# Samples' value products in rounds of four quarters, and the prompt's forget sums by tiles, in a fused two-layer encoder step

## The chip, the cores and the metric

The kernel runs on one core of one Trainium2 chip. The metric is the device time of one execution in microseconds (us). The engines are named as in the profile: PE is TensorE (matmul), PEld its weight loads, DVE VectorE, ACT ScalarE, POOL GpSimd, SP the engine that only issues DMAs. A time in the timeline is counted from the first instruction of the execution.

## The reference, cut to what matters

Two layers: a gated MLP with spatial mixing, then attention with a forget gate. Two request groups share the weights: a prompt of 512 rows, and 8 samples of 16 new rows, each with 256 cached rows of keys and values. There are 16 heads of 128. The change lies in the attention layer:

```python
def fox_attend_prompt(q, k, v, logf):
    cT = jnp.cumsum(logf, axis=1).transpose(0, 2, 1)      # running sums, per head
    ...
        s = jnp.einsum('bqhd,bkhd->bhqk', qi, k).astype(jnp.float32) * scale
        s = s + ci[..., :, None] - cT[:, :, None, :]
    ...

def fox_attend_sample(q, k_new, v_new, logf_new, k_cache, v_cache, logf_cache):
    k = jnp.concatenate([k_cache.astype(k_new.dtype), k_new], axis=1)
    v = jnp.concatenate([v_cache.astype(v_new.dtype), v_new], axis=1)
    ...
    p = jax.nn.softmax(s, axis=-1).astype(v.dtype)
    return jnp.einsum('bhqk,bkhd->bqhd', p, v).reshape(B, T, H * dh)
```

## The kernel before

All 640 rows (512 of the prompt, 128 of the samples) go through the layers together, as five tiles of 128. Large products are made from three products of halves: `mm3` splits each f32 operand into a high and a low part and adds high by high (L272), high by low (L273) and low by high (L274). The parts are written by `split`: ScalarE copies the high part (L289), VectorE subtracts it for the low part (L290, or L293 with a scale). The projections of the attention layer use seven products in place of eight (`seven_products`), whose operands are built by GpSimd (L211) and whose sums VectorE adds (L713 to L729).

The attention layer runs over eight pairs of heads. For each pair p the projections of the gate z of p and of v, k and q of p + 1 are a sequence of steps on TensorE, and pieces of attention are laid between them by written due times (`interleave`, `prompt_times`, `sample_times`). The program is then ordered by a scheduler that simulates the engines: an instruction is issued when it is ready in that simulation, unless `issue_after` ties it behind another. So the order around an edit can move too.

The prompt's pieces of a head are `scores`, `turn` (transposes of the softmax rows, L1186) and `values` (L1193), four blocks of 128 rows each. The samples' pieces of a pair and of a group of four samples are `scores` (L1243), `turn` (L1262), `values` (L1267 and L1270) and `gate` (L1277). A product of 32 output rows occupies one quarter of a PSUM bank's partitions; `bl` counts the four samples of a group, one to a quarter. `values` begins with one product over all 128 rows for the new rows' values, and then adds eight products of 32 rows for the cached values (two tiles t of 128 cached rows, four samples). So there are 16 executions of it, two to a pair.

`forget_sums` makes the running sums of the forget gate: four f32 products, one for each tile t of the prompt, with 16 rows (heads) as output and 512, 384, 256 and 128 columns. ScalarE copies them out (L1007), and they go to DRAM as `c_sc`, from where `load_w0` spreads one head's 512 sums over 128 partitions, once for each head. The first such load follows the store at once; its reader is VectorE's L1159. The samples' mask (`cs_sc`) is stored and loaded in the same place. At this place the program is in the projection of k and q of the first pair; L1016 and L1009 belong to the samples' sums, L1099 is the last step of `project_k0`, and L290 on `A` is the low half of a right operand, built from `sums[0]`.

Of the kernel before, what the change touches and what calls it, by code (L numbers as in the profile page):

```python
# [17 lines left out]
F32 = mybir.dt.float32  # L18
F32R = mybir.dt.float32r
AF = mybir.ActivationFunctionType  # L20
# [4 lines left out]
P = 128  # L25
D = 1024
E = 2048
H = 16
DH = 128
SEQ = 512  # L30
# [27 lines left out]
def hybrid_trunk(tc, x_prompt, x_sample, ck, cv, clf, p_prompt, p_sample, norm_pre, norm_post,  # L58
                 g_win, ln_g, ln_b, w_s, b_s, g_wout, f_win, b_f, f_wout, w_proj, w_gate, consts,
                 y_p, y_s, st_v, fk_p, fv_p, fl_p, fk_s, fv_s, fl_s):  # L60
    nc = tc.nc
# [7 lines left out]
    dram = tc.alloc_tile_pool(name="dram", bufs=1, space=DRAM)  # L69
# [13 lines left out]
    PB = [psum.tile([P, 512], F32, name=f"pb{i}") for i in range(8)]  # L83
    x_sc = dram.tile([NT, P, D], F32, name="x_sc")
    y_sc = dram.tile([H, P, TOK], F32, name="y_sc")
    c_sc = dram.tile([H, SEQ], F32, name="c_sc")
    cs_sc = dram.tile([P, 272], F32, name="cs_sc")
    rs_sc = dram.tile([16, P], F32, name="rs_sc")

    def r1(o, n, p=P):  # L90
        return R1[:p, o:o + n]
# [28 lines left out]
    def dma(out, in_, queue=None):  # L120
        if queue is not None:
            queue.dma_start(out=out, in_=in_)
        else:
            behind["sp"] = nc.sync.dma_start(out=out, in_=in_)
# [155 lines left out]
    tri = CST[:, C_TRI:C_TRI + 512]  # L280
# [332 lines left out]
    for p in range(4):  # L613
# [3 lines left out]
        out = v_out if p == 0 else [bank((0, 1, 2, 3, 4, 5, 6, 7)) for _ in range(NT)]  # L617
# [305 lines left out]
    o_KT, o_K, o_V, o_q, o_k, o_vk = 0, 2176, 3200, 5248, 6528, 7808  # L923
    o_P, o_PT, o_v, o_qp = 9088, 10112, 11136, 13696
# [27 lines left out]
    n = NT * H  # L952
    fx, fa, fe, fl, fu, lft = (r1(o_V + 1280 + z * n, n) for z in range(6))
    lf3 = lft.rearrange("p (t h) -> p t h", t=NT)
    fx3 = fx.rearrange("p (t h) -> p t h", t=NT)
    cT, ex, cS = r1(o_PT + 288, SEQ, H), r1(o_PT + 800, P), r1(o_V + 1760, 272)
    assert o <= o_K and o_PT + 288 >= o_P + 1280 and o_PTs + 96 >= o_qp + 1280

    def whole(i, j):
# [43 lines left out]
    def forget_sums():  # L1003
        pb = bank(ATT)
        for t in range(4):
            nc.tensor.matmul(pb[:H, t * P:], lf3[:, t], tri[:, :SEQ - t * P], start=(t == 0), stop=(t == 3))
        nc.scalar.activation(out=cT, in_=pb[:H, :], func=AF.Copy)  # L1007
        dma(c_sc, cT, nc.scalar)
        nc.vector.tensor_tensor(  # L1009
            out=ex.rearrange("p (r b h) -> p r b h", r=NB, b=NB),  # L1010
            in0=blk.rearrange("p (b r h) -> p r b h", b=NB, h=2),
            in1=lf3[:, 4, :].rearrange("p (r h) -> p r h", h=2).unsqueeze(2).broadcast_to([P, NB, NB, 2]), op=ALU.mult)
        pb = bank(ATT)
        nc.tensor.matmul(pb[:, :272], cr[:, 0], tri[:, :272], start=True, stop=False)
        nc.tensor.matmul(pb[:, P:272], cr[:, 1], tri[:, :272 - P], start=False, stop=False)
        nc.tensor.matmul(pb[:, 256:272], ex, CST[:, C_T16:C_T16 + TS], start=False, stop=True)  # L1016
        nc.scalar.activation(out=cS, in_=pb[:, :272], func=AF.Copy)
        behind["act"] = nc.scalar.dma_start(out=cs_sc, in_=cS)
        with queued("act"):
            load_w0(0, nc.scalar)  # L1020


    def v_of(p):
        return r1(o_v + (p % 2) * 1280, 1280).rearrange("p (t n) -> p t n", t=NT)
# [108 lines left out]
    def w0_of(h):  # L1133
        return tri if h % 2 else SF[:, 2048:2560] if h < 14 else r1(o_raw, 512)

    def load_w0(h, queue=None):
        dma(w0_of(h), c_sc[h].partition_broadcast(P), queue)

    def prompt_pieces(h):

# [60 lines left out]
    vv = r1(o_V, 2048).rearrange("p (b t n) -> p b t n", b=4, t=2)  # L1201
# [28 lines left out]
    def sample_pieces(p, bg):  # L1230

        pr = r1(o_Ps, 400)
        pt = r1(o_PTs, 384)
        os_ = r1(o_Ps, 256)
        kept = {}

        def scores():
            S = bank(ATT)
            with queued("dve"):
                nc.vector.tensor_tensor(out=Wc[:, PAST:], in0=Wc[:, PAST:], in1=CST[:, C_M16:C_M16 + TS], op=ALU.add)  # L1240
            for hh in range(2):
                for bl in range(4):
                    nc.tensor.matmul(S[32 * bl:32 * bl + 32, :272], qpads[:, hh, 4 * bg + bl].rearrange("p h q -> p (h q)"),  # L1243
                                     kt[:, hh, bl], start=(hh == 0), stop=(hh == 1))
            m, sm, ri = small(), small(), small()
            nc.vector.tensor_tensor_reduce(out=pr[:, :272], in0=S[:, :272], in1=Wc, scale=1.0, scalar=3e38, op0=ALU.add,
                                           op1=ALU.min, accum_out=m)
            nc.scalar.activation(out=pr[:, :272], in_=pr[:, :272], func=AF.Exp, scale=-1.0, bias=m, accum_out=sm)
            if 2 * p + bg < 15:
                load_mask(2 * p + bg + 1, nc.scalar)  # L1250
            nc.vector.reciprocal(out=ri, in_=sm)
            kept["ri"] = ri

            nc.vector.tensor_tensor(
                out=pr[:, 272:].rearrange("p (b k) -> p b k", b=NB),
                in0=CST[:, C_SEL + bg * P:C_SEL + (bg + 1) * P].rearrange("p (b k) -> p b k", b=NB),
                in1=pr[:, PAST:272].unsqueeze(1).broadcast_to([P, NB, TS]), op=ALU.mult)

        def turn():
            tb = bank(ATT)  # L1260
            for j, o_ in enumerate((0, P, 272)):
                nc.tensor.transpose(out=tb[:, j * P:(j + 1) * P], in_=pr[:, o_:o_ + P], identity=ident)  # L1262
            nc.scalar.activation(out=pt, in_=tb[:, :384], func=AF.Copy)

        def values():
            O = bank(ATT)
            nc.tensor.matmul(O[:, :256], pt[:, 256:], v_of(p)[:, 4], start=True, stop=False)  # L1267
            for t in range(2):
                for bl in range(4):
                    nc.tensor.matmul(O[32 * bl:32 * bl + 32, :256], pt[:, t * P + 32 * bl:t * P + 32 * bl + 32],  # L1270
                                     vv[:, bl, t], start=False, stop=(t == 1))
            nc.scalar.activation(out=os_, in_=O[:, :256], func=AF.Copy, scale=kept["ri"])

        def gate():
            tb = bank(ATT)
            for hh in range(2):
                nc.tensor.transpose(out=tb[:, hh * P:(hh + 1) * P], in_=os_[:, hh * P:(hh + 1) * P], identity=ident)  # L1277
            for hh in range(2):
                h = 2 * p + hh
                cs = slice(512 + 64 * bg, 512 + 64 * bg + 64)  # L1280
                y = y_of(h)[:, cs].rearrange("p (b q) -> p b q", b=4)
                o_ = tb[:, hh * P:(hh + 1) * P].rearrange("p (b h q) -> p b h q", b=4, h=2)[:, :, hh, :]
                nc.vector.scalar_tensor_tensor(out=y, in0=o_, scalar=0.5, in1=z_of(h)[:, cs].rearrange("p (b q) -> p b q", b=4),
                                               op0=ALU.mult, op1=ALU.mult)

        return scores, turn, values, gate
# [121 lines left out]
```

## Time and profile before

| | us |
|---|---|
| three runs | 1280.55, 1281.59, 1275.15 |
| their median | 1280.55 |
| the profiled execution, as timed | 1274.95 |
| its span, first to last instruction | 1273.1 |
| PE busy | 1265.6 (99%) |
| DVE busy | 957.5 (75%) |
| ACT busy | 595.3 (47%) |
| POOL busy | 353.3 (28%) |

The span is what the timeline covers; the time of the execution is 1.85 us longer. The granted clock of PE is 0.999 of full speed. PE's recorded durations overlap, since matmuls are pipelined and their ends are modelled; the distance between two starts is what a product takes of the sequence. An f32 product (not split in halves) is recorded twice, a transpose once.

### The profile page before, as it was taken

The numbers are of one execution on the slowest core, as the hardware profiler recorded it, in microseconds if no ns is written. First come the engines' busy times: TensorE is split into PE (matmuls) and PEld (weight loads), VectorE is DVE, ScalarE is ACT, GpSimd is POOL, SyncE is SP. The second block draws the span as 40 slices with busy tenths as digits, with TensorE's granted clock in tenths as the row PEclk, the third lists the DMA queues.
The fourth block names the chain that finished last, engine by engine and source line by source line (L and its number), as shares of the span: only waits on it lengthen the run. The fifth ranks groups of instructions, "written<-read, shape, count | busy, mean of one in ns | idle before, by whom it ended". The sixth has DMA issues, their size and how long they took to land.

```text
span 1273.1 us, 21241 instructions
## 1 busy us (share of the span) xinstructions
PE 1265.6 (99%) x7942; PEld 1138.3 (89%) x7942; DVE 957.5 (75%) x1795; ACT 595.3 (47%) x1076; POOL 353.3 (28%) x323
## 2 busy tenths in 40 slices
PE   9999999999999999999999999999999999999998
PEld 7888999999988888889999999999999999788887
DVE  6844999999943374799888898989888988545643
ACT  5424555444445253565445444545454545455331
POOL 1012445454000010155444434444435430000100
PEclk9999999999999999999999999999999999999999
DMA  5532343323324212658898758777888759632211
GB/s 204 177 102 67 112 125 120 92 88 98 121 85 161 88 35 87 150 125 174 159 169 169 185 150 187 164 164 143 152 162 179 178 114 287 221 129 83 67 66 50
DMA packets 275544, 171.52 MB, mean 135 GB/s; under 512 B 188721, under 2 KB 238689, under 8 KB 275442
## 3 DMA queue, kind: packets, MB, share of 16 engines
q1 hardware_dynamic: 261170, 127.80, 36.6%
q0 software_dynamic: 9760, 36.05, 14.0%
q10 hardware_dynamic: 4512, 6.33, 1.5%
q8 instruction: 62, 1.02, 0.3%
q14 instruction: 40, 0.33, 0.1%
HBM read 148.55 MB, written 21.59 MB: 134 GB/s over the span
## 4 chain that ended last, share of the span: by engine, by line
PE 98%; DVE 2%; DMA 0%; issue 0%; ACT 0%
PE pb L272 27%; PE pb L274 27%; PE pb L273 27%; PE pb L1193 3%; PE pb L419 2%; PE pb L1270 2%; PE pb L1186 1%; PE pb L1243 1%; PE pb L745 1%; PE pb L317 1%; PE pb L1058 1%; PE pb L1071 1%; PE pb L1267 1%; DVE W L290 0%; PE pb L1262 0%; PE pb L1059 0%
## 5 line engine op out<-in xcount | busy, mean ns | idle before, releaser
L272 PE MATMUL pb<-A,W 128*128 128x320 f32 (+1 forms) x752 | 240.8, 320 | 0.0
L273 PE MATMUL pb<-A,W 128*128 128x320 f32 (+1 forms) x752 | 233.8, 311 | 0.0
L274 PE MATMUL pb<-A,W 128*128 128x320 f32 (+1 forms) x752 | 233.3, 310 | 0.0
L290 DVE TENSOR_TENSOR W<-RAW,W 128x1024 fp32r<-128x1024 f32 (+1 forms) x122 | 146.1, 1198 | 73.0 <-ACT W L289 71.0
L273 PE MATMUL pb<-W,A 128*128 128x512 f32 x498 | 194.6, 391 | 0.0
L272 PE MATMUL pb<-W,A 128*128 128x512 f32 x498 | 194.6, 393 | 0.0
L274 PE MATMUL pb<-W,A 128*128 128x512 f32 x498 | 193.8, 392 | 0.0
L289 ACT ACTIVATE W<-RAW 128x1024 fp32r<-128x1024 f32 (+1 forms) x122 | 115.8, 949 | 87.9 <-PE pb L274 43.0
L272 PEld LDWEIGHTS pb<-A,W 128*128 128x128 f32 x752 | 141.7, 188 | 1.0 <-issue 0.2
L273 PEld LDWEIGHTS pb<-A,W 128*128 128x128 f32 x752 | 141.7, 188 | 0.5
L274 PEld LDWEIGHTS pb<-A,W 128*128 128x128 f32 x752 | 141.2, 188 | 0.0
L272 PE MATMUL pb<-tbf,W 128*128 128x320 f32 x360 | 119.0, 330 | 0.4 <-DVE R L1099 0.4
L303 POOL TENSOR_TENSOR SML<-SML 128x1 f32<-128x1 f32 x20 | 15.5, 777 | 349.8 <-DVE SML L301 345.0
L274 PE MATMUL pb<-tbf,W 128*128 128x320 f32 x360 | 111.4, 309 | 0.0
L273 PE MATMUL pb<-tbf,W 128*128 128x320 f32 x360 | 111.2, 309 | 0.0
L274 PEld LDWEIGHTS pb<-W,A 128*128 128x128 f32 x498 | 93.4, 188 | 19.3 <-issue 0.4
L273 PEld LDWEIGHTS pb<-W,A 128*128 128x128 f32 x498 | 93.6, 188 | 18.8
L272 PEld LDWEIGHTS pb<-W,A 128*128 128x128 f32 x498 | 93.5, 188 | 18.6
L211 POOL TENSOR_TENSOR sff<-RAW 128x512 f32<-128x512 f32 x46 | 60.9, 1324 | 177.4 <-DVE W L290 114.6
L713 DVE TENSOR_TENSOR R<-R,pb 128x320 f32<-128x320 f32 x184 | 86.5, 478 | 15.0 <-PE pb L274 13.7
L290 DVE TENSOR_TENSOR A<-R,A 128x640 fp32r<-128x640 f32 (+1 forms) x42 | 35.5, 880 | 57.6 <-ACT A L289 57.2
L272 PEld LDWEIGHTS pb<-tbf,W 128*128 128x128 f32 x360 | 67.8, 188 | 10.4 <-issue 6.6
(272 smaller groups left out, 2848.6 us busy)
## 6 DMA issues: line engine op xcount, KB each, us to landing
RAW<-in_fox_w_in POOLq DMA_DIRECT2D x46, 512.0 KB, 7.1
RAW<-in_gmlp_w_in SPq DMA_DIRECT2D x40, 512.0 KB
R<-in_cache_fox_k SPq DMA_DIRECT2D x128, 128.0 KB
R<-in_cache_fox_v SPq DMA_DIRECT2D x32, 512.0 KB
RAW<-in_gmlp_w_out SPq DMA_DIRECT2D x16, 512.0 KB
RAW<-in_ple_w_gate SPq DMA_DIRECT2D x16, 512.0 KB
RAW<-in_fox_w_out SPq DMA_DIRECT2D x16, 512.0 KB
R<-in_fox_w_in POOLq DMA_DIRECT2D x14, 512.0 KB, 7.8
```

The lines of the kernel that those rows point to most:

```text
L211: nc.gpsimd.tensor_tensor(out=o, in0=a, in1=b, op=op)
L272: nc.tensor.matmul(out, lh, rh, start=start, stop=False)
L273: nc.tensor.matmul(out, lh, rl, start=False, stop=False)
L274: nc.tensor.matmul(out, ll, rh, start=False, stop=stop)
L289: first = nc.scalar.activation(out=hi, in_=src, func=AF.Copy)
L290: nc.vector.tensor_tensor(out=lo, in0=src, in1=f(hi), op=ALU.subtract)
L303: behind["pool"] = nc.gpsimd.tensor_tensor(out=q, in0=t, in1=mhalf, op=ALU.pow)
L317: behind["pe"] = nc.tensor.transpose(out=b[:, j * P:(j + 1) * P], in_=src[:, (4 * c + j) * P:(4 * c + j + 1) * P], identity=ident)
L419: line[e] = make(*args, **kw)
L713: behind["dve"] = nc.vector.tensor_tensor(out=into(i, j), in0=a, in1=b, op=ALU.add)
L1193: nc.tensor.matmul(O[:, d], v[:, j, hh * P:(hh + 1) * P], pt[:, j * P:(j + 1) * P], start=(j == 0), stop=(j == i))
L1270: nc.tensor.matmul(O[32 * bl:32 * bl + 32, :256], pt[:, t * P + 32 * bl:t * P + 32 * bl + 32], vv[:, bl, t], start=False, stop=(t == 1))
```

## The change

The value products of a group of samples become twelve of 32 rows: the product with the new values is cut into four quarters too, and the twelve are issued tile by tile (new rows, then the two cached tiles), the four quarters after one another, each tied behind the one before. The running sums are made in tiles of 128 columns: tile g of the prompt goes to quarter g of the bank, and adds the tiles t up to g, so there are ten products of 32 rows (of which 16 are used) and 128 columns. `c_sc` becomes 128 x 128, with row 32 g + h for tile g and head h; the load of a head's sums gathers four rows of 128.

```diff
-    c_sc = dram.tile([H, SEQ], F32, name="c_sc")
+    c_sc = dram.tile([P, P], F32, name="c_sc")
...
-    cT, ex, cS = r1(o_PT + 288, SEQ, H), r1(o_PT + 800, P), r1(o_V + 1760, 272)
+    cT, ex, cS = r1(o_PT + 288, P), r1(o_PT + 800, P), r1(o_V + 1760, 272)
...
         for t in range(4):
-            nc.tensor.matmul(pb[:H, t * P:], lf3[:, t], tri[:, :SEQ - t * P], start=(t == 0), stop=(t == 3))
-        nc.scalar.activation(out=cT, in_=pb[:H, :], func=AF.Copy)
+            for g in range(t, 4):
+                nc.tensor.matmul(pb[32 * g:32 * g + 32, :P], lft[:, t * H:t * H + 32], tri[:, (g - t) * P:(g - t + 1) * P],
+                                 start=(t == 0), stop=(t == g))
+        nc.scalar.activation(out=cT, in_=pb[:, :P], func=AF.Copy)
         dma(c_sc, cT, nc.scalar)
...
     def load_w0(h, queue=None):
-        dma(w0_of(h), c_sc[h].partition_broadcast(P), queue)
+        dma(w0_of(h).rearrange("p (g n) -> p g n", g=4), c_sc.rearrange("(g h) n -> h g n", g=4)[h].partition_broadcast(P), queue)
...
         def values():
             O = bank(ATT)
-            nc.tensor.matmul(O[:, :256], pt[:, 256:], v_of(p)[:, 4], start=True, stop=False)
-            for t in range(2):
-                for bl in range(4):
-                    nc.tensor.matmul(O[32 * bl:32 * bl + 32, :256], pt[:, t * P + 32 * bl:t * P + 32 * bl + 32],
-                                     vv[:, bl, t], start=False, stop=(t == 1))
+            with ExitStack() as stack:
+                for t in (2, 0, 1):
+                    for bl in range(4):
+                        last = nc.tensor.matmul(O[32 * bl:32 * bl + 32, :256], pt[:, t * P + 32 * bl:t * P + 32 * bl + 32],
+                                                v_of(p)[:, 4] if t == 2 else vv[:, bl, t], start=t == 2, stop=t == 1)
+                        stack.enter_context(tc.issue_after(last.ins))
```

Lines below L1006 stand two or more lines lower in the changed file: L1186 is L1188 there, L1243 is L1245, the value products are L1272.

First place: PE, the value products of a pair's first group (pairs 1 to 6), with two of the prompt's turns between them. In the names, `pb` is a PSUM bank, `R_69` the large work tile. Before:

```order
L274 MATMUL pb_71<-A,W 128x320
L1267 MATMUL pb_74<-R_69 128x256
L1270 MATMUL pb_74<-R_69 32x256 x2
L1186 MATMUL pb_76<-CST,R_69 128x128 x2
L1270 MATMUL pb_74<-R_69 32x256 x6
L272 MATMUL pb_72<-tbf,W 128x320
```

After:

```order
L274 MATMUL pb_71<-A,W 128x320
L1272 MATMUL pb_74<-R_69 32x256 x4
L1188 MATMUL pb_76<-CST,R_69 128x128 x2
L1272 MATMUL pb_74<-R_69 32x256 x8
L272 MATMUL pb_72<-tbf,W 128x320
```

The turns stood behind two of the four quarters' products; they now stand behind four. In the first pair they stand behind three, and nine follow. In the second group of each pair, and in both groups of the last one, there is nothing between the products, before and after: 1 and 8 in a row, now 12.

Second place: PE, the running sums (L1006, now L1007) within the projection of q of the first pair. `tbf` and `A` are right operands, `W` weights. Before:

```order
L274 MATMUL pb_72<-tbf,W 128x320
L1006 MATMUL pb_74<-CST,R_69 16x512
L1006 MATMUL pb_74<-CST,R_69 16x384
L1006 MATMUL pb_74<-CST,R_69 16x256
L1006 MATMUL pb_74<-CST,R_69 16x128
L272 MATMUL pb_73<-A,W 128x320
L1016 MATMUL pb_75<-CST,R_69 128x16
L273 MATMUL pb_73<-A,W 128x320
```

After:

```order
L274 MATMUL pb_72<-tbf,W 128x320
L1007 MATMUL pb_74<-CST,R_69 32x128 x10
L1018 MATMUL pb_75<-CST,R_69 128x16
L272 MATMUL pb_73<-A,W 128x320
L273 MATMUL pb_73<-A,W 128x320
```

The ten products go to quarters 0 1 2 3, 1 2 3, 2 3 and 3, in this order; the samples' sum L1016 moved ahead of the projection's product. Thirteen products further the order changes too. Before, two products into bank `pb_71` stand ahead of the twelve into `pb_70`, which wait for VectorE's L1099, and ten follow them:

```order
L274 MATMUL pb_73<-A,W 128x320
L272 MATMUL pb_71<-A,W 128x320
L273 MATMUL pb_71<-A,W 128x320
L272 MATMUL pb_70<-tbf,W 128x320
L273 MATMUL pb_70<-tbf,W 128x320
```

After, all twelve into `pb_71` come first; the end of them and the start of `pb_70`:

```order
L272 MATMUL pb_71<-A,W 128x320
L273 MATMUL pb_71<-A,W 128x320
L274 MATMUL pb_71<-A,W 128x320
L272 MATMUL pb_70<-tbf,W 128x320
L273 MATMUL pb_70<-tbf,W 128x320
```

Ten products moved ahead of those that wait for L1099.

Third place: PE, the samples' first scores (L1243, now L1245) in the projection of z of the first pair. Before:

```order
L274 MATMUL pb_72<-A,W 128x320
L1243 MATMUL pb_74<-R_69 32x272 x8
L272 MATMUL pb_73<-tbf,W 128x320
```

After, the pair that moved and what follows it:

```order
L274 MATMUL pb_71<-tbf,W 128x320
L1245 MATMUL pb_74<-R_69 32x272 x2
L272 MATMUL pb_72<-A,W 128x320
L273 MATMUL pb_72<-A,W 128x320
L274 MATMUL pb_72<-A,W 128x320
```

The pair moved ahead of all twelve products into `pb_72`; the other six stand where the eight stood.

On the other engines the order moves little. On ACT the load of the mask (`cs_sc`) is issued ahead of the second bias load, and one bias load of each pair is issued ahead of the copy of the samples' values. On VectorE the reading of the first scores comes one weight split earlier. In the last stage, from the last pair's attention on, single products and copies change places.

## The prediction

> **What bounds the kernel now.** I read the page's engine shares first, then the chain that ended last, then what TensorE (PE) waits for, and only then single stretches of the timeline.
>
> ```profile
> span 1273.1 us, 21241 instructions
> PE 1265.6 (99%) x7942; PEld 1138.3 (89%) x7942; DVE 957.5 (75%) x1795; ACT 595.3 (47%) x1076; POOL 353.3 (28%) x323
> ...
> PE 98%; DVE 2%; DMA 0%; issue 0%; ACT 0%
> ```
>
> TensorE is busy from one end to the other and holds 98% of the chain. A busy PE need not be a PE at its peak, so I ask for its waits as well (waits of PE alone, longest first):
>
> ```profile
> PE pb L401 <- DVE r2a_t L393: 1.5, 1, 1.5
> PE pb L410 <- DVE r2a_t L419: 0.4, 1, 0.4
> PE pb L272 <- DVE R L1099: 0.4, 1, 0.4
> ```
>
> Together that is under 3 us in 1273, and the first two rows are the start of the kernel. So a change is worth what it takes off the sequence of starts on TensorE, and I cost it by start-to-start distances, not by the modelled durations, which overlap. The profiled execution took 1274.95 us (span 1273.1 and 1.85 around it); the median of the three runs is 1280.55, 5.6 above it, their spread 1275.15 to 1281.59. I sum against the profiled execution and carry the difference to the median.
>
> **1. The samples' value products.** They run 16 times. In 7 of them two of the prompt's turns (L1186) stand inside; the timeline of TensorE for one of these:
>
> ```profile
> 735.30 0.31 PE L274 MATMUL pb<-A,W 128*128 128x320 f32 x1
> 735.45 0.59 PE L1267 MATMUL pb<-R 128*128 128x256 f32 x2
> 735.97 0.62 PE L1270 MATMUL pb<-R 128*32 128x256 f32 x4
> 736.53 0.44 PE L1186 MATMUL pb<-CST,R 128*128 128x128 f32 x2
> 736.90 1.06 PE L1270 MATMUL pb<-R 128*32 128x256 f32 x12
> 737.89 0.41 PE L272 MATMUL pb<-tbf,W 128*128 128x320 f32 x1
> ```
>
> Each f32 product is recorded twice (two passes). The x4 row is two products in two quarters of the array: they take one round, 735.97 to 736.53, 0.56 us with the way back to full width. The x12 row is six products, of which four fit side by side and two are left: two rounds, 736.90 to 737.89, 0.99. One more round is thus 0.43, which is also what the full-width product costs (735.45 to 735.97, 0.52 with its change of width). Before: from the last L274 to L272 is 2.59 us, holding four such units (full, a half-filled round, a full round, a half-filled round). After: four products, the turns, eight products: three full rounds. For entering a round straight from full-width work and leaving it there is the samples' scores row:
>
> ```profile
> 583.84 0.31 PE L274 MATMUL pb<-A,W 128*128 128x320 f32 x1
> 584.08 1.12 PE L1243 MATMUL pb<-R 128*32 128x272 f32 x16
> 585.13 0.42 PE L272 MATMUL pb<-tbf,W 128*128 128x320 f32 x1
> 585.38 0.31 PE L273 MATMUL pb<-tbf,W 128*128 128x320 f32 x1
> ```
>
> Entering takes 0.24. After: 0.24 + 0.57 (one full round and out, 0.01 above the half-filled one) + 0.37 (the turns, 736.53 to 736.90) + 1.00 (two rounds and out) = 2.18, against 2.59: 0.41 less. This holds in six executions. In the first the order gives 3, turns, 9, so that the fourth quarter's product needs a round of its own: 0.24 + 0.57 + 0.37 + 1.43 = 2.61, nothing gained. In the other nine all products stand together:
>
> ```profile
> 631.29 0.31 PE L274 MATMUL pb<-A,W 128*128 128x320 f32 x1
> ...
> 631.97 1.07 PE L1270 MATMUL pb<-R 128*32 128x256 f32 x16
> 632.97 0.41 PE L272 MATMUL pb<-tbf,W 128*128 128x320 f32 x1
> ```
>
> 1.68 before; after 0.24 + 1.43 for three rounds and out = 1.67. A full-width pass and a round cost the same, so nothing is won there. Sum of the part: 6 x 0.41 = **-2.4 us**. Bounds: 0, if something else takes the place (below), and -2.9 with the first execution gaining too. I take -2.4, because the rows repeat to 0.01 us in this stage.
>
> The new tie makes each product queue behind the one ahead of it; all are TensorE's and stand in this order anyway, so it adds no wait. The turns come 0.42 earlier after the round's start than before. They need VectorE's L1180:
>
> ```profile
> 734.67 0.65 DVE L1180 TENSOR_SCALAR R<-R,SML 128x256 f32<-128x256 f32 x1
> ```
>
> It ends at 735.32; the turns would start at 735.30 + 0.24 + 0.57 = 736.11. 0.8 us of cover are left.
>
> The Trainium skill, "TensorE: Matmul & The Clock Gate" (section on packing small matmuls), states that a weight load overlaps with running matmuls only when its row group differs; quarters by columns share all rows, so by it the weights of each new round would be exposed. The trace differs: a second round adds 0.43, no more than a full-width product with hidden weights.
>
> **2. The running sums of the forget gate.** Before:
>
> ```profile
> 565.99 0.31 PE L274 MATMUL pb<-tbf,W 128*128 128x320 f32 x1
> 566.23 2.33 PE L1006 MATMUL pb<-CST,R 128*16 128x512 f32 x8
> 568.49 0.41 PE L272 MATMUL pb<-A,W 128*128 128x320 f32 x1
> 568.74 0.29 PE L1016 MATMUL pb<-CST,R 128*128 128x16 f32 x2
> 569.07 0.41 PE L273 MATMUL pb<-A,W 128*128 128x320 f32 x1
> ```
>
> Four products, one after the other, 2.26 us (566.23 to 568.49). After: ten of 128 columns in rounds of 4, 3, 2 and 1. The nearest row is the forget logits' last block, eight products of 128 columns in quarters, two rounds:
>
> ```profile
> 547.21 0.64 PE L968 MATMUL pb<-R,WF 128*32 128x128 f32 x16
> 547.78 0.33 PE L985 MATMUL pb<-CST,R 128*128 128x128 f32 x1
> ```
>
> 0.57 for two rounds and out. Four rounds are at most twice that, 1.14, and about 1.0 with the way out counted once. TensorE work falls by 1.26 (1.12 at least). But what comes next is not TensorE's. L273 multiplies by the low half that VectorE's L290 writes, and a later group of products waits for L1099 in the same queue (three rows of VectorE, then two of TensorE):
>
> ```profile
> 566.43 2.58 DVE L290 TENSOR_TENSOR A<-R,A 128x1280 fp32r<-128x1280 f32 x1
> 568.94 2.31 DVE L293 SCALAR_TENSOR_TENSOR W<-RAW,W 128x1024 fp32r<-128x1024 f32 x1
> 571.17 0.41 DVE L1099 TENSOR_TENSOR R<-R,pb 128x256 f32<-128x256 f32 x1
> 570.93 0.31 PE L273 MATMUL pb<-A,W 128*128 128x320 f32 x1
> 571.63 0.41 PE L272 MATMUL pb<-tbf,W 128*128 128x320 f32 x1 [0.39 <-DVE R L1099]
> ```
>
> L290 ends at 569.01 and L273 starts at 569.07: TensorE is already level with VectorE there, and nothing ahead of L290 on VectorE moves. I expect TensorE to arrive 1.2 us earlier and to wait 1.2 us at L273. The gain comes one step later: steps between these products are 0.15, and at 571.63 there is one of 0.70, 0.55 lost to L1099. The order now puts ten products (1.5 us) ahead of that group, which would start near 572.5, when L1099 is done. So **-0.55 us**; the bounds are 0 (the wait moves on) and -1.5 (VectorE is sooner done and all 1.26 arrive too). I take -0.55, the only one that needs no change on VectorE.
>
> ScalarE's copy of the sums shrinks from 16x512 to 128x128; TensorE does not wait for it, nothing counted.
>
> **3. The first scores.** In the first unit the order moves two of the eight score products ahead of a group of the projection. This pair takes a round of its own: 0.24 to enter, 0.59 for a round and out (1.05 of the row less 0.46 for the second round), 0.25 for the slower step behind it (585.13 to 585.38) = 1.08, in place of two steps of 0.15. The six that stay still take two rounds. **+0.78 us**; bounds 0.6 and, should the pair also stand before its operands are ready, 1.3.
>
> **4. The bias loads.** Each of 16 loads now has four pieces of 512 bytes per partition in place of one of 2 KB, and the mask's load is issued ahead of the second one. The page's line of packets, ScalarE's issue of the first load, and VectorE's rows around its reader:
>
> ```profile
> DMA packets 275544, 171.52 MB, mean 135 GB/s; under 512 B 188721, under 2 KB 238689, under 8 KB 275442
> ...
> 571.24 0.33 ACTq L122 DMA_DIRECT2D sff<-c_sc  x1
> ...
> 579.15 0.87 DVE L713 TENSOR_TENSOR R<-R,pb 128x320 f32<-128x320 f32 x2
> 579.95 0.28 DVE L1159 TENSOR_TENSOR R<-sff,CST 128x128 f32<-128x128 f32 x1
> 580.45 0.18 DVE L1240 TENSOR_TENSOR R<-R,CST 128x16 f32<-128x16 f32 x1 [0.23 <-DMA R<-cs_sc]
> ```
>
> 16 x 384 = 6144 packets more, 2% of all, with the same bytes. The first load has 8.7 us from issue to its reader L1159; later ones are issued a whole unit ahead. Counted as nothing. The last stage is ordered a little differently, with the same work: nothing, 0.2 either way.
>
> **Sum:** -2.4 - 0.55 + 0.78 = -2.2 us: 1272.8 for an execution like the profiled one, **1278.3** beside the median.
>
> **Rivals.**
> - *The sums' saving arrives whole* (VectorE is done earlier): another 0.95, 1277.4. Against it: L290 waits for nothing of TensorE's. 0.08.
> - *The rounds bring nothing*, since the turns wait in their new place: -2.2 + 2.4 = +0.2, 1280.7. It needs L1180 0.8 us later than it is. 0.06.
> - *New rounds expose their weights.* If each of the 16 added rounds showed two loads of about 0.1 (0.58 us for twelve loads by the row below, overlapped), 16 x 0.2 = 3.2, and the end is 1281.5. Against it, the 0.43 of part 1. 0.06. This is what the skill's rule of part 1 would give.
>
> ```profile
> 600.57 0.58 PEld L1270 LDWEIGHTS pb<-R 128*32 128x32 f32 x12 [0.17 <-issue]
> ```
>
> - *Slower: the first bias load comes late.* VectorE takes its work in order, so L1159 and all weight splits behind it would stand. TensorE's product at 585.13 uses a bank that VectorE emptied at 580.02 (L713), 5.1 us of cover. The load must come 14 us later than now to cost 8.6 and turn the sum to +0.5%. Four times the pieces at four times the 8.7 us would be 26 late, 21 lost: near 1299. Against it: keys arrive in much smaller pieces all through this stage. 0.04.
> - *The runs themselves.* One of three runs is 5.4 below the median. If the changed kernel's median falls there, 1275.15 - 2.2 = 1273.0. 0.19.
>
> The forecast itself has 0.57. **Numbers.** 0.5% is 6.4 us, the spread of the three runs; less cannot be told from no change. Faster: the fast runs, 0.19. Slower: the late load, 0.04. The rest, 0.77, is within 0.5%. The range takes in the lowest run less 3.1 (1272.0) and the highest with the exposed weights (1281.59 + 1.0, 1282.6).
>
> **What would show it.** Eight and sixteen records around the turns in six executions, 2.18 from L274 to L272; nine executions with 24 records unchanged at 1.67; the sums in about 1.0 us, with L273 still about 0.05 behind the end of L290 and no wait for L1099; 1.08 for the pair of scores. Wrong would be: new waits of PE on VectorE or on a load in the unit after the sums, rounds above 0.43, or L290 ending earlier.

## The result and the profile after

The change makes the kernel slower. Changed: median 1296.34 us of six runs (1287.3 to 1307.16); before, on the same chip: 1277.70 of six (1275.11 to 1281.59). The ratio is 1.0140, with a 95% interval of 1.0118 to 1.0163. The highest execution, 1307.16, lies over 1.5% above the lowest and is left out of the ratio; the median of the other five is 1294.94. The profiled execution took 1298.97, its span 1297.1. From the page of the changed kernel (span, busy times, the line of packets, ScalarE's DMA queue):

```profile
span 1297.1 us, 21457 instructions
...
PE 1270.6 (98%) x8050; PEld 1139.7 (88%) x8050; DVE 963.5 (74%) x1795; ACT 594.8 (46%) x1076; POOL 357.8 (28%) x323
...
DMA packets 281801, 171.57 MB, mean 132 GB/s; under 512 B 188721, under 2 KB 247009, under 8 KB 281698
...
q10 hardware_dynamic: 10000, 6.37, 2.4%
```

The span grew by 24.0 us and TensorE's modelled busy time by 5.0, so most of the loss is waiting. The packets grew by 6257, the bytes by 0.05 of 171.52 MB. What TensorE waits for, the longest of it (in total, times, longest):

```profile
PE pb L272 <- DVE SML L1174: 9.3, 2, 7.3
PE pb L1188 <- DVE R L1182: 6.5, 5, 2.8
```

Before, no wait behind the start of the kernel was longer than 0.4. VectorE is late because it waits itself. Its longest waits for transfers behind the start of the kernel, first before, then after ("issue" names no releaser; the reader in that row is the transpose of cached keys):

```profile
DVE R L726 <- DMA out<-R: 1.8, 1, 1.8
DVE R L1219 <- DMA R<-in_cache_fox_k: 0.5, 1, 0.5
...
DVE R L1240 <- DMA R<-cs_sc: 0.2, 1, 0.2
```

```profile
DVE R L1221 <- issue: 5.8, 1, 5.8
DVE R L1221 <- DMA R<-in_cache_fox_k: 5.5, 3, 4.4
DVE R L726 <- DMA out<-R: 4.0, 1, 4.0
```

The transposes of the samples' cached keys (L1219 before, L1221 after) stood 0.5 us in all, and now 11.3 (5.5 of it by the named load, 5.8 without a name). The worst place is the first unit after the sums; TensorE and its granted clock there, and two rows behind the stall:

```profile
605.30 0.69 PE L272 MATMUL pb<-W 128*128 128x384 f32 x1 [7.26 <-DVE SML L1174]
...
606.43 0.47 PE L273 MATMUL pb<-tbf,W 128*128 128x320 f32 x1
606.70 0.47 PE L274 MATMUL pb<-tbf,W 128*128 128x320 f32 x1
```

```profile
600.00:605.00 5.00, 0.00 (x0) 0.00 (x0) 3.57 (x10) 0.00 (x0) 0.74 (x1) 0.64 0.26 46
605.00:607.00 2.00, 1.70 (x6) 1.70 (x7) 2.00 (x6) 1.92 (x6) 1.92 (x2) 0.50 1.10 172
607.00:609.00 2.00, 2.00 (x12) 2.00 (x12) 2.00 (x2) 0.26 (x1) 1.92 (x2) 0.69 0.03 4
```

(The columns of the second fence: the stretch, its length, busy time of PE, PEld, DVE, ACT and POOL, then the granted clock, the DMA engines' share, GB/s.) The stall also costs what comes behind it: the clock falls to 0.50, and steps that took 0.15 take 0.27, until 608.28.

### The profile page after: what moved, and what is told of

It reads as the page before. It is cut to its first block, busy times and chain, and to the rows that moved or that the text cites. A ratio compares the mean times of both kernels' runs of the same rounds, so it can differ in the third digit from the quotient of the medians.

```text
span 1297.1 us, 21457 instructions
## 1 busy us (share of the span) xinstructions
PE 1270.6 (98%) x8050; PEld 1139.7 (88%) x8050; DVE 963.5 (74%) x1795; ACT 594.8 (46%) x1076; POOL 357.8 (28%) x323
## 5 line engine op out<-in xcount | busy, mean ns | idle before, releaser
L272 PE MATMUL pb<-A,W 128*128 128x320 f32 (+1 forms) x752 | 241.2, 321 | 0.3 <-DVE R L729 0.3
L274 PE MATMUL pb<-A,W 128*128 128x320 f32 (+1 forms) x752 | 233.4, 310 | 0.0
L290 DVE TENSOR_TENSOR W<-RAW,W 128x1024 fp32r<-128x1024 f32 (+1 forms) x122 | 149.5, 1226 | 72.4 <-ACT W L289 70.6
L272 PE MATMUL pb<-W,A 128*128 128x512 f32 x498 | 195.0, 394 | 2.2 <-DVE R L729 1.2
L274 PE MATMUL pb<-W,A 128*128 128x512 f32 x498 | 194.3, 391 | 0.0
L272 PEld LDWEIGHTS pb<-A,W 128*128 128x128 f32 x752 | 141.9, 189 | 1.7 <-DVE R L729 0.5
L274 PEld LDWEIGHTS pb<-A,W 128*128 128x128 f32 x752 | 141.5, 188 | 0.0
L272 PE MATMUL pb<-tbf,W 128*128 128x320 f32 x360 | 119.3, 332 | 0.0
L272 PEld LDWEIGHTS pb<-W,A 128*128 128x128 f32 x498 | 93.5, 188 | 21.6 <-issue 1.4
L211 POOL TENSOR_TENSOR sff<-RAW 128x512 f32<-128x512 f32 x46 | 61.5, 1338 | 184.0 <-DVE W L290 88.3
L274 PE MATMUL pb<-tbf,W 128*128 128x320 f32 x360 | 111.8, 310 | 0.0
L274 PEld LDWEIGHTS pb<-W,A 128*128 128x128 f32 x498 | 93.4, 188 | 19.6 <-issue 0.4
L290 DVE TENSOR_TENSOR A<-R,A 128x640 fp32r<-128x640 f32 (+1 forms) x42 | 35.5, 880 | 60.5 <-ACT A L289 60.5
L272 PEld LDWEIGHTS pb<-tbf,W 128*128 128x128 f32 x360 | 68.1, 189 | 10.2 <-issue 7.5
```

The lines of the kernel that those rows point to most:

```text
L211: nc.gpsimd.tensor_tensor(out=o, in0=a, in1=b, op=op)
L272: nc.tensor.matmul(out, lh, rh, start=start, stop=False)
L274: nc.tensor.matmul(out, ll, rh, start=False, stop=stop)
L290: nc.vector.tensor_tensor(out=lo, in0=src, in1=f(hi), op=ALU.subtract)
```

## The experiments

Every ratio is to the kernel before on the same chip in the same series, whose median was 1275.5 to 1276.8 in the four series.

| kernel | us, median (range, runs) | ratio, 95% interval |
|---|---|---|
| e1, value rounds alone | 1273.19 (1272.62–1279.85, 9) | 0.9979, 0.9963–0.9994 |
| e2, change, loads in one piece | 1279.62 (1277.62–1280.96, 12) | 1.0020, 1.0009–1.0031 |
| e3, before, loads in four pieces | 1289.98 (1286.16–1291.10, 4) | 1.0096, 1.0076–1.0116 |
| e4, change without value rounds | 1291.70 (1290.78–1294.12, 4) | 1.0118, 1.0099–1.0136 |
| e5, e2, one weight load 0.8 us later | 1277.63 (1274.31–1280.21, 10) | 1.0012, 1.0002–1.0022 |
| e6, e3, last two loads by ScalarE | 1294.45 (1290.83–1297.25, 4) | 1.0144, 1.0121–1.0167 |
| e7, e3, mask loaded first | 1303.38 (1292.51–1309.36, 4) | 1.0206, 1.0152–1.0260 |
| e8, before, two pieces of 1 KB | 1280.09 (1275.12–1282.76, 10) | 1.0017, 0.9997–1.0037 |
| e9, e2, two weight loads 2.5–4 us later | 1276.73 (1275.37–1279.34, 10) | 1.0003, 0.9992–1.0013 |
| e10, e1 and those two loads later | 1275.25 (1273.95–1277.02, 10) | 0.9984, 0.9970–0.9998 |
| e11, before, eight pieces of 256 bytes | 1298.38 (1295.74–1301.03, 2) | 1.0170, 1.0136–1.0203 |
| e12, e3, pieces 17 rows apart, not 32 | 1276.45 (1275.03–1280.27, 10) | 1.0011, 0.9999–1.0022 |
| e13, the change, rows padded to 528 bytes | 1279.55 (1277.15–1283.00, 10) | 1.0026, 1.0011–1.0041 |
| e14, e13 with the weight load of e5 | 1276.00 (1274.98–1280.35, 10) | 1.0008, 0.9998–1.0018 |

**e1: the value rounds alone.** The kernel before, with the new `values` of the change.

```diff
-            nc.tensor.matmul(O[:, :256], pt[:, 256:], v_of(p)[:, 4], start=True, stop=False)
-            for t in range(2):
...
+                for t in (2, 0, 1):
+                    for bl in range(4):
...
+                        stack.enter_context(tc.issue_after(last.ins))
```

> The kernel before with the value products in twelve tied quarters alone; sums, store and loads as before. Theory A (the bias loads in 512-byte pieces hold up the other transfers): no loss here, 2.4 us faster than before, 1275.3 beside 1277.7; no wait of PE on VectorE's L1180 or L1172. Theory B (the moved order of the program costs the time): about 0, the order outside the value products is that of before. Theory C (the turns now come before VectorE is ready): waits at L1186 as in the changed kernel, 6.5 us in total, so 4 us slower than before.

Faster by 2.7 us at the medians. The timeline of TensorE at the turns, the place of the prediction's first fence:

```profile
735.10 0.31 PE L274 MATMUL pb<-A,W 128*128 128x320 f32 x1
735.34 0.64 PE L1270 MATMUL pb<-R 128*32 128x256 f32 x8
735.90 0.44 PE L1186 MATMUL pb<-CST,R 128*128 128x128 f32 x2
736.27 1.07 PE L1270 MATMUL pb<-R 128*32 128x256 f32 x16
737.27 0.41 PE L272 MATMUL pb<-tbf,W 128*128 128x320 f32 x1
```

From L274 to L272 it is 2.17, against 2.59 before. The turns wait for nothing. This is also the fastest version of all that were run.

**e3: the pieces alone.** The kernel before, but `c_sc` in rows of 128, and each bias load of four pieces; the same instructions in the same order on every engine.

```diff
-    c_sc = dram.tile([H, SEQ], F32, name="c_sc")
+    c_sc = dram.tile([P, P], F32, name="c_sc")
-        dma(c_sc, cT, nc.scalar)
+        dma(c_sc.rearrange("(g h) n -> h g n", g=4)[:H], cT.rearrange("p (g n) -> p g n", g=4), nc.scalar)
-        dma(w0_of(h), c_sc[h].partition_broadcast(P), queue)
+        dma(w0_of(h).rearrange("p (g n) -> p g n", g=4), c_sc.rearrange("(g h) n -> h g n", g=4)[h].partition_broadcast(P), queue)
```

> The kernel before with one edit: the sums lie in DRAM as four rows of 128 for each head, so that each of the 16 bias loads has four pieces of 512 bytes per partition; every engine's order is that of before. Theory A: all of the loss, 1293 to 1300 (the forecast gain is missing), with VectorE waiting for the loads of the cached keys and the stores. Theory B and theory C: no change, 1277 to 1279.

14.1 us slower, from the layout of one small DRAM tile: a little less than theory A's loss, and at other waits than those it names. Since the order is the same, the starts of TensorE's 7942 records can be set against each other one by one: of 11.2 us in this profiled execution (1286.16, the fastest of its four), 5.0 are lost between 587 and 605, and 5.0 at 1079. The first place is VectorE at the samples' mask, whose load stands behind the two bias loads in ScalarE's queue; the second is ScalarE waiting for `y_sc`, which SP issued behind a bias load, and then TensorE:

```profile
586.33 0.17 DVE L1240 TENSOR_TENSOR R<-R,CST 128x16 f32<-128x16 f32 x1 [5.91 <-DMA R<-cs_sc]
```

```profile
1074.52 0.74 ACT L289 ACTIVATE A<-R 128x640 fp32r<-128x640 f32 x1 [5.59 <-DMA R<-y_sc]
```

```profile
1078.98 1.32 PE L272 MATMUL pb<-W,A 128*128 128x512 f32 x2 [2.62 <-DVE R L729]
```

SP's stores of new keys, issued meanwhile, are slow too: the four that were issued within 4.77 us before take 10.63 (SP's timeline, before and e3), and all that SP does next comes 6 us later.

```profile
574.12 4.77 SPq L124 DMA_DIRECT2D out<-R  x4
```

```profile
574.31 10.63 SPq L124 DMA_DIRECT2D out<-R  x4
```

**e2 and e4: the rest of the change.** e2 is the whole change with loads of one piece (four stores put the quarters of the bank side by side in `c_sc`); e4 is the change with the old `values` (e1's diff the other way round).

```diff
-    c_sc = dram.tile([P, P], F32, name="c_sc")
+    c_sc = dram.tile([H, SEQ], F32, name="c_sc")
-        dma(c_sc, cT, nc.scalar)
+        for g in range(4):
+            dma(c_sc[:, g * P:(g + 1) * P], cT[32 * g:32 * g + H], nc.scalar)
-        dma(w0_of(h).rearrange("p (g n) -> p g n", g=4), ...)
+        dma(w0_of(h), c_sc[h].partition_broadcast(P), queue)
```

> The whole change, except that the sums lie in DRAM as before (16 rows of 512): ScalarE stores each quarter's 16 heads by a transfer of its own, and each bias load is one piece of 2 KB per partition again. Theory A: the loss of 18 us goes, and what was forecast is left, about 1275.5 beside 1277.7 (2.2 us faster). Theory B: most of the loss stays, 1290 or more, since pair of scores and sums are ordered as in the change. Theory C: 4 to 6 us of waits at the turns stay, near 1281.

> The change without the new value products: sums by tiles in quarters and bias loads in four pieces. Theory A: as the changed kernel without the 2.4 us of the rounds, 1296 to 1300. Theory B: the same, since the order around the sums is that of the change. Theory C: no loss, 1277 to 1280.

e4 shows that 15.8 us are lost without the value rounds. Whether the rounds add something beside the slow loads stays open: by e1's gain the whole change should lose less than e4, but its ratio is 1.0140 against 1.0118 (the intervals overlap). e2 shows that the pieces are not all of the loss: 3.7 us slower where the sum said 2.2 faster, so some 6 us have another cause. (In e2 the eight first scores stand together again, so part 3's 0.78 is not in it.) It is not theory C's: the turns wait once in e2, for 1.0. VectorE there waits once for cached keys, and TensorE for VectorE:

```profile
596.78 1.42 DVE L1222 STREAM_TRANSPOSE R<-R 128x256 f32<-128x256 f32 x4 [4.66 <-DMA R<-in_cache_fox_k]
```

```profile
600.65 0.69 PE L272 MATMUL pb<-W 128*128 128x384 f32 x1 [4.50 <-DVE SML L1175]
```

**e5, e9 and e10: the race of weights and keys.** GpSimd's timeline, before and in e2, shows a move that I had not read: the load of the weights to `R` now stands ahead of the last operand sum (L211).

```profile
585.69 1.30 POOL L211 TENSOR_TENSOR sff<-RAW,sff 128x512 f32<-128x512 f32 x1
586.94 0.77 POOL L122 DMA_DIRECT2D RAW<-in_fox_w_in  x1
587.70 0.75 POOL L122 DMA_DIRECT2D R<-in_fox_w_in  x1
```

```profile
586.05 0.77 POOL L122 DMA_DIRECT2D R<-in_fox_w_in  x1
586.85 1.31 POOL L211 TENSOR_TENSOR sff<-RAW,sff 128x512 f32<-128x512 f32 x1
588.08 0.77 POOL L122 DMA_DIRECT2D RAW<-in_fox_w_in  x1
```

SP issues the cached keys from 585 on, at the same time. e5 ties that one load behind the sum again; e9 ties both loads behind the next sum; e10 does the same to e1. The order on every engine stays otherwise.

```diff
...
+                if state["raw"] == S2 + 11:      # e5; S2 + 11 and S2 + 12 in e9 and e10
+                    stack.enter_context(tc.issue_after(state["sum"].ins))
...
```

> The change with bias loads of one piece, as in the second experiment, with one instruction moved: on GpSimd's queue the weight load R<-in_fox_w_in of 586.05 stands behind the last operand sum (L211) again, about 2 us later, where it stood before the change. Theory W: that load, moved ahead, takes the DMA engines before the cached keys issued at 585.76 to 588.7 have landed; so VectorE stood 4.66 us at the transposes of the keys, and TensorE 4.5. Then the wait and the stall go: 1279.6 - 4.5 = 1275.1 us. Theory S: the keys are late because the five stores of ScalarE's queue (three more than before) and the earlier load of v push SP's queue back; then the stall stays and the time is 1279.6.

> The change with bias loads of one piece (second experiment, 1279.6), and on GpSimd's queue the two weight loads R<-in_fox_w_in and RAW<-in_fox_w_in of 586 to 588.9 now stand behind the next operand sum (L211), at about 590, when the cached keys of 585.8 have landed. Nothing else moves on any engine. Theory W: keys and weights race for the DMA engines, and whoever comes first in the rings delays the other; moved by 0.8 us only (fifth experiment) the times fell to between 1274.3 and 1280.2, some executions winning the race and some not. With 2.5 us more the keys always win: no wait of VectorE at the transposes of the keys, no stall of 4.5 us of TensorE, and nearly all executions near 1273.5 (e1's 1273.2 and +0.2 for sums and scores). Against that, the weights land 2 us later; GpSimd waited 7.7 us for them before, so a new wait of up to 2 us behind its sums is possible: 1275.5. Theory S: the keys are late for another reason (the stores of the sums, the place of the load of v); then 1279.

> The kernel before with the tied rounds of the value products alone (first experiment, 1273.2, with one execution of nine at 1279.9), and the same two weight loads moved behind the next operand sum. By theory W the kernel before loses the same race in some executions (those of 1279 to 1282 among its 1275s); moved, the high executions go and the median stays: 1273.0 to 1273.5, all below 1275. If the weights are missed there, 1274 to 1275.5 in all.

e5 came out between the theories: 1.5 us above the kernel before where e2 was 3.7 above it (the intervals overlap), with single executions from 1274.31 to 1280.21. The profiled one is the slowest of them, and there VectorE still waited 5.90 for the keys. In e9's profiled execution the keys come in time, VectorE waits 0.34 there in place of 4.66, and the stall of 4.5 is gone; in its place the weights are late:

```profile
PE pb L1198 <- DVE R L1192: 2.6, 1, 2.6
```

So theory W has the mechanism, and its fear came true as well: e9 is level with the kernel before (1276.73 against 1276.78), and the 1273.5 to 1275.5 expected are missed. e10 has the same new wait (1.6) and gains 1.5 over the kernel before, where e1 gained 2.7. Its highest execution is 1277.0, where the kernel before went up to 1282.4 in the same series; that those high executions are lost races too would fit, but no run shows it.

**e6 and e7: where the pieces hurt.** e6 is e3 with the last two bias loads moved to ScalarE's queue, e7 is e3 with the load of the mask ahead of the first two.

```diff
-            pieces += [(48, lambda: load_w0(14)), (48, lambda: load_w0(15))]
+            pieces += [(48, lambda: load_w0(14, nc.scalar)), (48, lambda: load_w0(15, nc.scalar))]   # e6: by ScalarE, not SP
```

```diff
...
+            behind["act"] = nc.scalar.dma_start(out=Wc, in_=cs_sc[:8].unsqueeze(1).broadcast_to([8, TS, 272]))   # e7: the mask, then load_w0(0)
...
```

> The kernel before with bias loads of four pieces, as in the third experiment (1290.0), but the last two of them (heads 14 and 15) go by ScalarE's queue and not by SP's. Theory Q: in the last unit the pieces hold up what stands behind them in SP's own queue, up to the loads of y_sc and the weights of the last projection, which costs 2.9 us at 1079 and 2 more in slow steps behind it; then that stall goes, and the time is 1285. Theory E: pieces hold the DMA engines themselves, whatever queue they come by; then the stall stays, and the time is 1290. The stall of 5.2 in the first unit stays in both.

> The kernel before with bias loads of four pieces, as in the third experiment (1290.0), with the load of the samples' mask put ahead of the first two bias loads on ScalarE's queue, and these two in the order of heads. VectorE's wait of 5.91 us for the mask at L1240 goes in any case. Theory M: the mask alone made the loss of 5.2 us in the first unit; then the time is 1290 - 4 = 1286 (about 1 left, for the first bias load lands behind the mask). Theory K: the cached keys of the second group are late as well, since every transfer behind the pieces lands 6 us later; then VectorE waits at the transposes of the keys (L1219 in the profile before) for about what it no longer waits for the mask, 4 to 5 us, and the time stays at 1290.

In e6 the wait for `y_sc` and its stall are gone, but the time did not fall. TensorE now stands 2.57 us at 1079.66, eleven microseconds earlier in the program, because the weights of the last projection are late: SP issues them behind sixteen stores, which take 13.27 us to issue while the last load's pieces, by ScalarE's queue, run beside them (8.00 in e3); one store alone stands 4.88.

```profile
1057.27 13.27 SPq L124 DMA_DIRECT2D out<-R  x16
```

So theory Q had the place right and not the cause: pieces hold up other queues' transfers too, as theory E says. (This execution is the slowest of e6's four; waits of TensorE of 4.24 in the first unit and 4.63 at 952.7, behind VectorE at the transposes of cached keys, came on top.) In e7 the wait for the mask is gone, but VectorE's next waits are 4.70 for the first bias load and 3.35 at the keys. That does not decide between theories M and K: e7 issues the first bias load 10.9 us later than e3 does (at 571.42 there), while ScalarE stands 10.68 us for a store of SP's:

```profile
582.27 0.38 ACTq L122 DMA_DIRECT2D sff<-c_sc  x1
```

VectorE's order and the place of two other loads moved a little too, so e7's time measures neither the mask nor the pieces.

**e8, e11 and e12: why the pieces are slow.** All three are e3 with another layout. In e3 the four pieces of a head lie 32 rows of 512 bytes apart, 16 KB (128 rows in four quarters). e8 has two pieces of 1 KB, 16 KB apart; e11 eight of 256 bytes, 4 KB apart; e12 four of 512 bytes, 17 rows or 8.5 KB apart. (The expectation of e12 below puts e3's pieces 16 rows apart; by e3's layout it is 32, so e12 nearly halves the distance.)

```diff
-    c_sc = dram.tile([P, P], F32, name="c_sc")
+    c_sc = dram.tile([32, 2 * P], F32, name="c_sc")   # e8
+    c_sc = dram.tile([P, 64], F32, name="c_sc")     # e11
+    c_sc = dram.tile([68, P], F32, name="c_sc")     # e12: 17 rows to a quarter, of which 16 are used
```

> The kernel before with bias loads of two pieces of 1 KB in place of one of 2 KB. Theory P: a load's time goes by the number of its pieces. The first two loads take 4.4 us with 256 pieces and 13.2 with 1024; with 512 they take about 7.3, so the mask comes 2 to 3 us late, some 0.8 of it covered, and the last stage loses less than a third of its 5; 1275.9 + 2 to 4, so 1278 to 1280. Theory B: only pieces under 1 KB are slow; then nothing is lost and the time is 1275.9. Theory D: any load with a second dimension is slow, whatever the size of its pieces; then it is 1290 as with four.

> The kernel before with bias loads of eight pieces of 256 bytes. Theory P (time by the number of pieces): from the issue of the first to the last packet of the first two loads it took 4.1 us with 256 pieces, 6.3 with 512 and 12.9 with 1024; with 2048 it takes 22 to 26. The mask then lands about 10 us later than with four pieces, and the first unit loses 15 in place of 5; with the last unit in proportion, 1310 to 1325. Theory B (a floor by the size of a piece, reached at 512 bytes, so that smaller ones go no slower in bytes): the same bytes in half the size are no slower than twice as many packets of keys of 128 bytes, which pass at over 1000 per us here; then 1290 as with four.

> The kernel before with bias loads of four pieces of 512 bytes, as in the third experiment (1290.0), but the four pieces of a head lie 17 rows of 512 bytes apart in DRAM, and not 16. Same packets, same order on every engine. While the first two loads run, DRAM gives a rate that doubles with the piece: about 44 GB/s with pieces of 256 and of 512 bytes, 87 with 1 KB, 174 to 200 with 2 KB. Theory C: it is not the number or size of the pieces but where they lie: pieces 4, 8 or 16 KB apart are served by the same part of the memory, 44 GB/s for each part, and 2 KB in a row are four parts. Then 17 rows give four parts again, the two loads take 4 to 5 us and not 12.9, the stall at L1240 and the later ones go, and the time is 1276 to 1277. Theory P (pieces of 512 bytes are slow by themselves): 1290.

At its median e8 agreed with the count of pieces (4.0 us slower, though its interval takes in no change), e11 with neither theory: twice the packets, and the two first loads take 13.8 us from issue to last packet, against 12.9 with four pieces, 6.3 with two and 4.1 with one (5.7 in e12). The answer is in the rate. Two microseconds of each inside these loads (the DMA view; before, two, four, eight pieces, and last e12):

```profile
DMA packets 258, 0.46 MB, mean 231 GB/s; under 512 B 23, under 2 KB 44, under 8 KB 258
```

```profile
DMA packets 165, 0.17 MB, mean 84 GB/s; under 512 B 1, under 2 KB 165, under 8 KB 165
```

```profile
DMA packets 177, 0.09 MB, mean 45 GB/s; under 512 B 0, under 2 KB 177, under 8 KB 177
```

```profile
DMA packets 336, 0.09 MB, mean 43 GB/s; under 512 B 336, under 2 KB 336, under 8 KB 336
```

```profile
DMA packets 595, 0.30 MB, mean 149 GB/s; under 512 B 14, under 2 KB 595, under 8 KB 595
```

With pieces of 256 bytes 4 KB apart and of 512 bytes 16 KB apart the rate is the same 43 to 45 GB/s; with 1 KB, 16 KB apart, twice that; and with the same four pieces of 512 bytes 8.5 KB apart it is 149, and 13.2 of the 14.1 us are gone. So number and size alone do not make the loss; the place of the pieces does. A round distance alone doesn't either: rows of cached keys lie 8 KB apart, in pieces of 128 bytes, and pass at 173 GB/s (before, 568 to 570):

```profile
DMA packets 2742, 0.35 MB, mean 173 GB/s; under 512 B 2742, under 2 KB 2742, under 8 KB 2742
```

But each of those pieces is read once, while all 128 partitions read the same four pieces of a bias load. That this is the difference is argued, not shown. Theory C's parts of the memory fit these rates roughly; what the memory does inside no run shows. The Trainium skill, "DMA: Bandwidth & Descriptors" (section "Latency and other measured facts"), has a loss of the kind for rows 2 to 8 MiB apart, cured by 4 KiB of padding and not by 192 bytes; here 16 KB is far enough apart for one, and 512 bytes cure it (e13).

**e13 and e14: the whole change, with the place mended.** e13 differs from the change only in the rows of `c_sc`, 528 bytes long, so that a head's pieces lie 33 times 512 bytes apart (16.5 KB) and not 32 times; e14 ties GpSimd's weight load as e5 does.

```diff
-    c_sc = dram.tile([P, P], F32, name="c_sc")
+    c_sc = dram.tile([P, 132], F32, name="c_sc")
-        dma(c_sc, cT, nc.scalar)
+        dma(c_sc[:, :P], cT, nc.scalar)
...
```

> The whole change as it is (1296.3), with rows of c_sc padded from 512 to 528 bytes, so that the four pieces of a head lie 33 times 512 bytes apart and not 32 times. Same packets, same order. Theory C: the 14 us of the pieces go, the race of weights and cached keys stays (GpSimd's load of weights still stands ahead): 1276 to 1280, as the second experiment's 1279.6, or lower, since the sums are one store and not four. Theory P: 1296.

> As the run before this, with GpSimd's weight load R<-in_fox_w_in behind the last operand sum, as in the fifth experiment. By theory C with theory W: the race of keys and weights is as in the kernel before, and the time is e1's 1273.2 and 0.2 for sums and scores: 1273 to 1275; executions that lose the race, 1278 to 1280. By theory P: 1294.

e13 came as theory C said; e14's median is 1.0 above the 1273 to 1275 expected. Two microseconds inside e13's first two loads (in the changed kernel, 573 to 575, it is 44 GB/s):

```profile
DMA packets 558, 0.35 MB, mean 173 GB/s; under 512 B 16, under 2 KB 555, under 8 KB 558
```

The change with its loads mended is 4.0 us slower than before, as e2 was (3.7), and with GpSimd's load behind its sum again it is nearly level (0.5; the two intervals just overlap). Each against the kernel before of its series, e14 is still 3.2 behind e1, where the terms for sums and scores say 0.2; its profile shows TensorE waiting 1.1 at 601.6 for VectorE and 0.5 for a cached v at 671. The rest of that is not settled.

## Why the prediction was wrong, point by point

**Part 1, the value products (-2.4): right.** e1 measured -2.7, its interval 0.8 to 4.7; 2.17 at the turns where 2.18 was worked out; and the nine executions without turns stand at 1.43 for three rounds:

```profile
631.75 1.50 PE L1270 MATMUL pb<-R 128*32 128x256 f32 x24
633.18 0.41 PE L272 MATMUL pb<-tbf,W 128*128 128x320 f32 x1
```

So the new rounds show no exposed weights in their time, and the rule weighed there does not hold for these products.

**Part 2, the sums (-0.55): the mechanism right.** The changed kernel, TensorE and then VectorE:

```profile
567.19 1.08 PE L1007 MATMUL pb<-CST,R 128*32 128x128 f32 x20
568.20 0.40 PE L1018 MATMUL pb<-CST,R 128*128 128x16 f32 x2
568.44 0.39 PE L272 MATMUL pb<-A,W 128*128 128x320 f32 x1
570.03 0.41 PE L273 MATMUL pb<-A,W 128*128 128x320 f32 x1 [1.19 <-DVE A L290]
```

```profile
567.38 2.59 DVE L290 TENSOR_TENSOR A<-R,A 128x1280 fp32r<-128x1280 f32 x1
```

1.01 us for the ten products, then a wait of 1.19 until 0.06 behind the end of L290, and no wait for L1099 any more. The 0.55 by itself was not timed.

**Part 3, the first scores (+0.78): the size right.** The pair takes 0.24 to enter, 0.58, and 0.25 behind it, 1.07 where 1.08 was forecast:

```profile
582.15 0.31 PE L274 MATMUL pb<-tbf,W 128*128 128x320 f32 x1
582.39 0.65 PE L1245 MATMUL pb<-R 128*32 128x272 f32 x4
582.97 0.41 PE L272 MATMUL pb<-A,W 128*128 128x320 f32 x1
583.22 0.30 PE L273 MATMUL pb<-A,W 128*128 128x320 f32 x1
```

**Part 4, the bias loads ("Counted as nothing"): this step failed.** It cost 14.1 us (e3). I reasoned with the count of packets ("2% of all, with the same bytes") and a cover of 8.7 us for the first reader. The count was right (6257 packets more where I counted 6144; q10 went from 4512 to 10000) and said nothing: these loads pass at 45 GB/s in place of 231. And the cover was the wrong one to ask for: L1159 itself was not late in e3; the mask behind it in ScalarE's queue was, and SP's stores and its load of `y_sc`, which have no 8.7 us.

**The rival "the first bias load comes late", at 0.04, had the right load and the wrong wait.** It gave 1299, and the profiled execution took 1298.97, but that is luck. Its reader (L1159, now L1161) waits neither in e3 nor in the changed kernel. Its 26 us took the 8.7 from issue to reader as the load's own time, and the two first loads had landed 4.1 after the issue. And what it lost at one place is lost at several, a part of it by the order. Its chance was cut by "keys arrive in much smaller pieces all through this stage". That row was true and did not bear on it: the keys pass at 173 GB/s in the same stage, each piece read by one partition only. A row for the same kind of transfer, one short row spread to 128 partitions from several places, was not in the trace, and its cost should have stood with both ends: 0, and the rival's 21.

**The order: a term was missing.** I followed the moves on TensorE, ScalarE and VectorE and wrote that on the other engines little moves. GpSimd's weight load, moved ahead by one sum, and SP's load of v, moved ahead of stores, were in the order too; with both weight loads later, e9 is 3.8 us better than e2, each against the kernel before of its series; the rest of e2's 6 us is not settled.

**The sum, put right.** Taken out of the whole change one after the other, the causes measure so at the medians: 18.6 us slower as it is (17.2 without the highest execution), 4.0 with the place of the pieces mended (e13), 0.5 with the weight load tied back as well (e14). The forecast was 2.2 faster, so 2.7 stay open. The losses measured one by one do not simply add: 14.1 for the pieces (e3) and about 6.4 for the order (e2's 3.7 and the 2.7 it hides) make 20.5, and e4, which has both, lost 15.8. In e4's profile VectorE stands once for the cached keys, 6.7: that both causes delay these same keys, and so overlap, fits this, but is not shown.

## What to carry to other kernels

When a change lays out a small DRAM tile anew, look at where the pieces of one load lie: a row spread to all partitions from pieces 4 or 16 KB apart ran here at a fifth to a little over a third of its rate, and 16 bytes of padding to each row gave most of it back. Ask of a slower load not only when its own reader comes, but what is queued behind it on its queue and on the others. And where a scheduler sets the order, read the queues that issue transfers on every engine, GpSimd's and SP's too, for two loads that are wanted at the same time.

## What the runs showed of the hardware

A stall of TensorE of 2.6 us and more cost more than its length here. Two pieces (e8): a wait of 2.73 us at 600.06, and then the granted clock (columns: the stretch, its length, busy PE, clock, DMA share, GB/s):

```profile
600.00:602.00 2.00, 1.94 (x9) 0.69 1.02 161
602.00:604.00 2.00, 2.00 (x10) 0.50 0.10 15
```

In the start-by-start comparison with the kernel before, the steps behind this stall lost another 1.6 us by 604.2. Waits of 1.6 us (e10) and 2.1 us (e13) were followed by no such steps, the clock staying at 1.00. The Trainium skill, "TensorE: Matmul & The Clock Gate" (section "What's actually happening"), gives half the clock after an idle window of about 3.4 us; the half clock agrees, but here 2.6 to 2.7 us of waiting were enough (e3, e8 and e9).

A row in DRAM that all partitions read came at 231 GB/s in one piece, and at 43 to 45 in four pieces 16 KB apart or eight 4 KB apart; four pieces 8.5 KB apart gave 149 (e12), and 16.5 KB apart 173, another load included (e13). While such a load runs, transfers of other queues are held up too (SP's four stores took 10.63 us to issue in e3 in place of 4.77, its sixteen 13.27 in e6 in place of 8.00), though its packets keep the DMA engines busy for a fourth of the time only (22.5% in the two microseconds of e3 above).
